# A hybrid decoder layer on one core: preparing the query weights beside four heads instead of two, and another order of the query products

## The chip, the core and the metric

The kernel runs on one core of a Trainium2 chip. The metric is device time in microseconds (us): the kernel before took 1506.83 us, the median of 3 runs (1504.25 to 1510.64). The engines are named as the profile names them: PE is TensorE (matmuls), DVE is VectorE, ACT is ScalarE, POOL is GpSimd, and SP is the engine on whose queue nearly all DMA transfers are issued.

## The reference: what is computed

One decoder layer over 1024 tokens of width 1024, in float32. Cut to what matters:

```python
h  = rmsnorm(x, ln1) @ w_in          # q, k, v and gates of all heads
m1 = mlstm_chunkwise(...)            # 4 heads of width 128, after a causal convolution and silu
m2 = forgetting_attention(...)       # 8 heads of width 64
x  = x + concat(m1 * out_gate, m2) @ w_out
h  = rmsnorm(x, ln_x)
q  = h @ w_xq                        # 4 heads of width 256
k, v = split(rmsnorm(mem, ln_mem) @ w_kv)          # 256 memory tokens
x  = x + (softmax(q @ k.T / 16) @ v) @ w_xo
x  = rmsnorm(x + relu(rmsnorm(x) @ w1) ** 2 @ w2)
```

The change touches two places: the mLSTM heads, beside which the weights w_xq are prepared, and the stretch from q to the first tiles of the product with w_xo.

## The kernel before, in words

**Precision and tiles.** Every float32 operand is split into a high and a low part (`split`, lines 141 and 142: ACT copies the high part, DVE subtracts the low one; with a scale, lines 144 and 145), and a product takes three matmuls (`mm3`, lines 195 to 197). A full tile of the output, 128 x 512, takes 8 x 3 = 24 matmuls. The accumulator banks are named mm, tp, m2 (the profile writes m), sc and ov. A bank must be evacuated, mostly by DVE, before the next product may start in it. Working tiles come from pools with few buffers: `w4` (5 buffers of 128 x 1024), `act` (7 of 128 x 4096 values, which `quarters` cuts into four of 128 x 1024), `w2` (half tiles with a letter each; r_a has one buffer only), and the weights' wr (2 buffers), wh and wl (3 each).

**Order.** The order of instructions on PE, ACT, DVE and POOL is set by a scheduler from the program's order, and each engine then takes its instructions strictly in that order. SP issues its DMAs in order as well, so an issue that waits for a buffer holds up those behind it.

**The query weights.** The product q = h @ w_xq is taken by a scheme with seven products of quarters instead of eight. For it, sums and differences of the quarters of the weights are formed ahead of time, split, and kept in DRAM (`leftd`). `query_parts(c, kh)` does this for one of eight parts (c is the head, 0 to 3, kh a half of the rows) in two phases: first two loads of w_xq (L701), a split of three quarters (128 x 768) and two stores (L706); then four additions of 128 x 256 (L711), a split of 128 x 1024, and two stores (L715). `ml_project(hd)` projects one mLSTM head and calls four parts' phases in between, in heads 1 and 3 only (the list `ahead`); heads 0 and 2 have none.

**The mLSTM head.** Its projections run one after the other on PE (convolution of k, `fx_project(0, hd)` for the attention's queries, `carried`, convolution of q, `fx_project(1, hd)`, `carry`, output gate), while the head before it is closed piece by piece (`closing`). To close it, a factor for each of its 1024 tokens is computed on DVE (c_fac, to line 673), transposed on PE, stored to DRAM (`facd`, L273) and loaded again, broadcast to all partitions, in two halves (r_a, L275 and L683); line 686 multiplies by it. `fx_project` evacuates its bank in line 724 (r_p).

**The query stage.** A list, `plan`, written out by hand, gives the order of: the loads of left operands (`L`), the query products `C(c, i)` (line 195 on; twelve matmuls each, i from 1 to 7; sums are formed on DVE in line 1281, into r_d, r_e, r_f and r_p, and a bank is used by several of these products in turn), the splitting of the right operands (`cut_right`, `cut_fourth` with the subtractions of line 1254), the loads of the memory's keys and values (`K`), the folding of a sum of squares into the factors of the second norm (`rsqrt_sums`: two additions in line 250, then four matmuls in line 253), the attention over the memory (`X`), and the start of the product with w_xo. The sums of squares themselves are formed by accumulating DMAs on POOL's queue (row<-r_c, line 1229), one for each tile of the stage before.

**The start of w_xo.** The attention's results of heads 0 to 2 go to DRAM (osd) and are loaded and split as operands (`os_load`, `os_split`). `begin_xo(n)` starts output tile n with the 18 matmuls of the six chunks that are there; `end_xo` adds the six of the last head. Three tiles are begun, in banks mm, m2 and sc. Others are computed in one go (`first_half`).

## Time and profile before

| what | value |
|---|---|
| device time, median of 3 runs | 1506.83 us (1504.25 to 1510.64) |
| the profiled execution | 1506.87 us |
| its span, from first to last instruction | 1505.1 us |
| granted clock of PE, mean | 0.995 |
| PE busy | 1481.2 us (98%) |
| DVE busy | 1140.3 us (76%) |
| ACT busy | 739.3 us (49%) |

Times in the views count from the start of the span; the execution's own time is 1.8 us longer. The projections of the mLSTM heads lie at about 65 to 345 us, the query products up to about 745 us (the last sum of line 1281 at 745.4), and the first output tiles from 749 us on. A row of waits names the engine, the line that waited, what it waited for, and the time. In a timeline, brackets behind a row hold the idle time before it and who ended it. The granted clock is 1.00 where PE runs at full speed.

### The profile page before, as it was taken

Reading aid. Unit: us, or ns where it says so; the run is one execution under the profiler, and the core shown is the slowest. Engines: PE = TensorE matmul, PEld = TensorE weight load, DVE = VectorE, ACT = ScalarE, POOL = GpSimd, SP = SyncE. Lnnn points to the kernel's source line nnn. Section 1 sums busy time; section 2 is a strip of 40 time slices with the busy share of each in tenths; the row PEclk is TensorE's granted clock in tenths of the full one; section 3 lists DMA queues with packets and bytes.
Section 4 is the critical chain, followed back from the end, with each engine's and each line's share of the span. In section 5 each row is a group of like instructions: output and inputs, shape, how many; then the busy total and the mean of one; then the engine's idle time right before and its main releaser. Section 6 shows DMA issues by size and latency. Waiting matters only on the chain.

```text
span 1505.1 us, 22082 instructions
## 1 busy us (share of the span) xinstructions
PE 1481.2 (98%) x7620; PEld 1241.3 (82%) x7620; DVE 1140.3 (76%) x1844; ACT 739.3 (49%) x1385; POOL 455.0 (30%) x545
## 2 busy tenths in 40 slices
PE   9999999999999999999999999999999999999997
PEld 8888788889999888778878788788887788888887
DVE  7687787976798875663468988888877788777765
ACT  7343344444688764533454556665656332222134
POOL 0002031313466552111110043443443653343312
PEclk9999999999999999999999999999999999999998
DMA  6345744687989768965656447767776965555623
GB/s 210 109 146 163 229 148 151 224 265 202 291 246 269 207 214 305 332 195 162 213 179 204 140 146 249 264 248 269 266 246 241 347 251 217 223 223 224 252 84 112
DMA packets 142116, 326.11 MB, mean 217 GB/s; under 512 B 15522, under 2 KB 44508, under 8 KB 136116
## 3 DMA queue, kind: packets, MB, share of 16 engines
q1 hardware_dynamic: 139700, 320.92, 62.9%
q0 software_dynamic: 2016, 3.67, 1.4%
q8 instruction: 60, 0.98, 0.3%
q14 instruction: 52, 0.43, 0.1%
q10 hardware_dynamic: 288, 0.11, 0.0%
HBM read 208.52 MB, written 112.45 MB: 213 GB/s over the span
## 4 chain that ended last, share of the span: by engine, by line
PE 77%; DMA 9%; DVE 7%; ACT 3%; issue 3%; POOL 1%; SPq 1%; POOLq 0%; DVEq 0%; ACTq 0%
PE tp L195 6%; PE tp L196 6%; PE tp L197 6%; PE sc L195 6%; PE sc L196 6%; PE sc L197 6%; PE mm L195 5%; PE mm L196 5%; PE mm L197 5%; PE m L195 5%; PE m L196 5%; PE m L197 5%; PE ov L899 2%; PE tp L879 2%; PE ov L195 2%
## 5 line engine op out<-in xcount | busy, mean ns | idle before, releaser
L195 PE MATMUL tp<-act,wl 128*128 128x512 f32 (+1 forms) x440 | 172.3, 392 | 2.5 <-DVE wl L142 1.3
L196 PE MATMUL tp<-act,wh 128*128 128x512 f32 (+1 forms) x440 | 172.3, 392 | 0.0
L197 PE MATMUL tp<-act,wh 128*128 128x512 f32 (+1 forms) x440 | 171.7, 391 | 0.0
L141 ACT ACTIVATE wh<-wr 128x1024 fp32r<-128x1024 f32 (+3 forms) x80 | 75.6, 946 | 76.0 <-PE tp L197 28.2
L195 PE MATMUL mm<-act,wl 128*128 128x512 f32 (+1 forms) x284 | 109.1, 384 | 3.1 <-DVE r_p L724 2.6
L196 PE MATMUL mm<-act,wh 128*128 128x512 f32 (+1 forms) x280 | 107.4, 383 | 0.5 <-DVE act L142 0.5
L197 PE MATMUL mm<-act,wh 128*128 128x512 f32 (+1 forms) x280 | 107.2, 383 | 0.0
L196 PE MATMUL sc<-act,wh 128*128 128x512 f32 (+1 forms) x276 | 106.8, 387 | 0.0
L197 PE MATMUL sc<-act,wh 128*128 128x512 f32 (+1 forms) x276 | 106.8, 387 | 0.0
L195 PE MATMUL sc<-act,wl 128*128 128x512 f32 (+1 forms) x268 | 104.1, 388 | 0.0
L196 PE MATMUL m<-act,wh 128*128 128x512 f32 (+1 forms) x268 | 102.0, 380 | 0.0
L197 PE MATMUL m<-act,wh 128*128 128x512 f32 (+1 forms) x268 | 101.8, 380 | 0.0
L195 PEld LDWEIGHTS tp<-act,wl 128*128 128x128 f32 x440 | 82.7, 188 | 22.4 <-ACT row L1664 1.7
L142 DVE TENSOR_TENSOR wl<-wr,wh 128x1024 fp32r<-128x1024 f32 (+3 forms) x80 | 91.7, 1147 | 11.5 <-ACT wh L141 11.4
L197 PEld LDWEIGHTS tp<-act,wh 128*128 128x128 f32 x440 | 82.7, 188 | 19.1
L196 PEld LDWEIGHTS tp<-act,wh 128*128 128x128 f32 x440 | 82.7, 188 | 18.6
L1741 POOL TENSOR_TENSOR z<-wr 128x256 f32<-128x256 f32 x56 | 54.2, 989 | 143.2 <-DMA wr<-w_ff2q 70.2
L195 PE MATMUL m<-act,wl 128*128 128x512 f32 (+1 forms) x256 | 97.5, 381 | 0.0
L141 ACT ACTIVATE w<-wr 128x768 fp32r<-128x768 f32 (+2 forms) x31 | 25.5, 824 | 130.4 <-PE tp L197 69.0
L141 ACT ACTIVATE wh<-z 128x1024 fp32r<-128x1024 f32 (+2 forms) x55 | 52.5, 957 | 64.2 <-POOL z L1741 32.2
L142 DVE TENSOR_TENSOR wl<-z,wh 128x1024 fp32r<-128x1024 f32 (+2 forms) x55 | 66.9, 1219 | 12.3 <-ACT wh L141 12.3
L195 PEld LDWEIGHTS mm<-act,wl 128*128 128x128 f32 x284 | 53.7, 189 | 14.3 <-DVE r_p L724 3.0
(789 smaller groups left out, 4413.8 us busy)
## 6 DMA issues: line engine op xcount, KB each, us to landing
act<-right SPq DMA_DIRECT2D x35, 1024.0 KB
right<-r_d SPq DMA_DIRECT2D x70, 256.0 KB
right<-w SPq DMA_DIRECT2D x56, 256.0 KB
wr<-w_ff2q SPq DMA_DIRECT2D x28, 512.0 KB
act<-fqk SPq DMA_DIRECT2D x48, 256.0 KB
wr<-w_in SPq DMA_DIRECT2D x20, 512.0 KB
wr<-w_ff SPq DMA_DIRECT2D x20, 512.0 KB
fqk<-r_p SPq DMA_DIRECT2D x32, 256.0 KB
```

Of the source, the lines that this page charges most:

```text
L141: s.activation(hi, src, AF.Copy)
L142: return v.tensor_tensor(out=lo, in0=src, in1=hi.bitcast(F32), op=ALU.subtract)
L195: nc.tensor.matmul(ps, w[1], x[0], start=first, stop=False, skip_group_check=more)
L196: nc.tensor.matmul(ps, w[0], x[1], start=False, stop=False, skip_group_check=more)
L197: nc.tensor.matmul(ps, w[0], x[0], start=False, stop=last, skip_group_check=more)
L879: nc.tensor.transpose(self.ps[:, d * P : (d + 1) * P], self.pts[d][:, self.j * P : (self.j + 1) * P], ident)
L899: nc.tensor.matmul(self.ov[:, c0:], self.fv[:, self.j], t[:, c0:], start=self.j == 0 and t is self.p[1], stop=self.last and t is self.p[0])
L1741: g.tensor_tensor(out=o, in0=x, in1=y, op=op)
```

## The change

Three edits. First, every head now carries two parts of the query weights in four phases: one inside `fx_project(0, hd)`, between its two tiles, one behind it, one behind `fx_project(1, hd)`, and one between the two tiles of the output gate. Even heads take the four working tiles of a part out of one act tile (`quarters`), odd heads take four w4 tiles. Second, the plan takes the products of the first two heads in turn, (0, 3), (1, 3), (0, 6), then cut_fourth, (1, 6), (0, 7), (1, 7), with the foldings of the two sums behind (0, 7) and (1, 7), and some loads and attention steps move by a place or two. Third, two output tiles are begun, not three; the third is computed in one go after them.

```diff
-    def query_parts(c, kh):
-
-        r = w4()
+    def query_parts(c, kh, rooms):
+
+        r, hi, lo, hs = rooms()
...
-    def fx_project(which, n):
+    def fx_project(which, n, between=lambda: None):
...
+            if hf == 0:
+                between()
...
-        ahead = [query_parts(*divmod(4 * (hd // 2) + i, 2)) for i in range(4)] if hd % 2 else []
-
-        def step(i):
-            if ahead:
-                next(ahead[i])
+        rooms = (lambda: [w4() for _ in range(4)]) if hd % 2 else quarters
+        ahead = [x for kh in range(2) for x in [query_parts(hd, kh, rooms)] * 2]
+
+        def step():
+            next(ahead.pop(0))
...
-        fx_project(0, hd)
+        fx_project(0, hd, step)
+        step()
         next(closing, None)
         parts = carried(hd, yk)
-        step(0)
         next(closing, None)
         state = []
         yq = conv_silu(hd, *q, lambda: state.extend(states(hd, *parts)))
-        step(0)
-        step(1)
         fx_project(1, hd)
-        step(1)
-        step(2)
+        step()
         sums = carry(hd, q, yq, *state)
-        step(2)
-        step(3)
...
-        step(3)
+            if hf == 0:
+                step()
```

Of the plan, the lines that matter here:

```diff
-        *C((0, 3)), O(cut_fourth), *C((1, 3)), K(0, 0, "wh"), K(0, 1, "wl"), O(rsqrt_sums, second_acc[0], rcol[:, 0:4], 4, 1, None, None, rsqrt_cols, True), *C((0, 6)), O(rsqrt_sums, second_acc[1], rcol[:, 4:8], 4, 1, None, None, rsqrt_cols, True), *C((0, 7)),
-        *C((0, 4)), L(2, 1, "wr"), X(0, 1), *C((1, 6)), L(2, 2, "wr"), L(2, 6, "wh"),
+        *C((0, 3), (1, 3)), K(0, 0, "wh"), K(0, 1, "wl"), *C((0, 6)), O(cut_fourth), *C((1, 6), (0, 7)), O(rsqrt_sums, second_acc[0], rcol[:, 0:4], 4, 1, None, None, rsqrt_cols, True), *C((1, 7)), O(rsqrt_sums, second_acc[1], rcol[:, 4:8], 4, 1, None, None, rsqrt_cols, True),
+        *C((0, 4)), L(2, 1, "wr"), X(0, 1), L(2, 2, "wr"), L(2, 6, "wh"),
...
-        O(begin_xo, 0), X(3, 0), X(3, 1), O(begin_xo, 1), X(3, 0), O(begin_xo, 2), X(3, 1), O(end_xo, 0), X(3, 1), O(end_xo, 1), O(end_xo, 2), *S(1, 0, 2, 4),
+        O(begin_xo, 0), X(3, 0), X(3, 1), O(begin_xo, 1), X(3, 0), X(3, 1), O(end_xo, 0), X(3, 1), O(end_xo, 1), O(first_half, 2), *S(1, 0, 2, 4),
```

The line numbers of the change are one to four lower behind the first edits (724 becomes 723, 1254 becomes 1251, 1281 becomes 1278). At three places the order of DVE is needed later.

DVE in head 1, around the two multiplications by the reloaded factors (L686, r_a) and the evacuation of bank mm (r_p<-mm); z is the convolution, before:

```order
L546 SCALAR_TENSOR_TENSOR z_223_1723<-z_215_1641,vec,z_223_1723 128x1024
L593 SCALAR_TENSOR_TENSOR r_p_1669<-r_p_1669,c_mx_1593 128x128
L546 SCALAR_TENSOR_TENSOR z_223_1723<-z_215_1641,vec,z_223_1723 128x1024
L686 SCALAR_TENSOR_TENSOR r_f_1207<-r_f_1207,vec,r_a_1507 128x512
L546 SCALAR_TENSOR_TENSOR z_223_1723<-z_215_1641,vec,z_223_1723 128x1024
L687 SCALAR_TENSOR_TENSOR r_f_1207<-w_140_1230,r_f_1207 128x512
L724 SCALAR_TENSOR_TENSOR r_p_1781<-mm_1756,row 128x512
L142 TENSOR_TENSOR wl_2179<-wr_2176,wh_2178 128x1024
L591 TENSOR_TENSOR r_p_1669<-sc_1681,r_p_1669 128x128
L686 SCALAR_TENSOR_TENSOR r_f_1208<-r_f_1208,vec,r_a_1590 128x512
```

And with the change:

```order
L686 SCALAR_TENSOR_TENSOR r_f_1229<-r_f_1229,vec,r_a_1537 128x512
L546 SCALAR_TENSOR_TENSOR z_226_1762<-z_218_1680,vec,z_226_1762 128x1024
L593 SCALAR_TENSOR_TENSOR r_p_1708<-r_p_1708,c_mx_1641 128x128
L687 SCALAR_TENSOR_TENSOR r_f_1229<-w_142_1252,r_f_1229 128x512
L591 TENSOR_TENSOR r_p_1708<-sc_1720,r_p_1708 128x128
L686 SCALAR_TENSOR_TENSOR r_f_1230<-r_f_1230,vec,r_a_1638 128x512
L593 SCALAR_TENSOR_TENSOR r_p_1708<-r_p_1708,c_mx_1641 128x128
L549 SCALAR_TENSOR_TENSOR z_226_1762<-z_218_1680,z_226_1762 128x1024
L145 SCALAR_TENSOR_TENSOR r_f_1229<-r_f_1229,r_y_1633 128x512
L687 SCALAR_TENSOR_TENSOR r_f_1230<-w_142_1252,r_f_1230 128x512
L723 SCALAR_TENSOR_TENSOR r_p_1802<-mm_1777,row 128x512
```

The evacuation stood behind the first of the two multiplications and ahead of the second; now it stands behind both. The last phase of query parts that stood ahead of these rows, and that of the next part, are gone from here.

DVE in the query stage, around the evacuation of bank mm after product (0, 6) (r_d<-mm) and the two subtractions of cut_fourth (w<-act) with their splits, before:

```order
L1254 TENSOR_TENSOR w_1378_7595<-act_4004 128x1024
L1254 TENSOR_TENSOR w_1379_7596<-act_4004 128x1024
L142 TENSOR_TENSOR act_7576<-w_1260_6938,act_7576 128x1024
L145 SCALAR_TENSOR_TENSOR w_1366_7530<-sc_7443,w_1366_7530 128x512
L142 TENSOR_TENSOR act_7599<-w_1378_7595,act_7599 128x1024
L142 TENSOR_TENSOR act_7599<-w_1379_7596,act_7599 128x1024
L1281 TENSOR_TENSOR r_d_7593<-sc_7537,r_p_7328 128x512
L1281 TENSOR_TENSOR r_d_7593<-mm_7635,r_d_7593 128x512
```

And with the change:

```order
L1278 TENSOR_TENSOR r_e_7538<-sc_7525,r_p_7316 128x512
L142 TENSOR_TENSOR act_7540<-act_3992,act_7540 128x1024
L142 TENSOR_TENSOR act_7564<-w_1248_6926,act_7564 128x1024
L145 SCALAR_TENSOR_TENSOR w_1354_7518<-sc_7431,w_1354_7518 128x512
L1278 TENSOR_TENSOR r_d_7581<-sc_7525,r_p_7316 128x512
L1278 TENSOR_TENSOR r_d_7581<-mm_7601,r_d_7581 128x512
L1278 TENSOR_TENSOR r_e_7558<-ov_7545,r_p_7444 128x512
L1251 TENSOR_TENSOR w_1371_7618<-act_3992 128x1024
L1251 TENSOR_TENSOR w_1372_7619<-act_3992 128x1024
```

The two subtractions stand behind the evacuation now, and the splits of what they form behind them.

DVE a few rows on, around the evacuation of bank m2 after product (1, 6) (r_d<-m) and the fold of the second sum (L250), before:

```order
L1281 TENSOR_TENSOR r_e_7550<-mm_7635,r_e_7550 128x512
L145 SCALAR_TENSOR_TENSOR w_1394_7678<-r_e_7550,w_1394_7678 128x512
L1281 TENSOR_TENSOR r_d_7616<-ov_7557,r_p_7456 128x512
L1281 TENSOR_TENSOR r_d_7616<-m_1403_7742,r_d_7616 128x512
L250 TENSOR_TENSOR row<-row 64x256 x2
L1281 TENSOR_TENSOR r_p_7328<-mm_7635,r_p_7328 128x512
```

And with the change:

```order
L1278 TENSOR_TENSOR r_d_7595<-ov_7545,r_p_7444 128x512
L250 TENSOR_TENSOR row<-row 64x256
L1278 TENSOR_TENSOR r_d_7595<-m_1374_7627,r_d_7595 128x512
L250 TENSOR_TENSOR row<-row 64x256
L145 SCALAR_TENSOR_TENSOR w_1375_7641<-r_d_7595,w_1375_7641 128x512
```

Both folds stood behind that evacuation; now the first of them stands ahead of it. On PE, product (1, 7), which uses bank m2 next, came behind product (0, 4) and 18 matmuls of scores; now it comes behind (0, 4) and four small matmuls, and the 18 come after it.

More of the change, by code (lines that the diff above doesn't have):

```diff
@@ L701, in query_parts @@
             load(q[:, 2 - 2 * e : 4 - 2 * e], a["w_xq"][2 * c + e].rearrange("p (j h c) -> h p j c", j=2, h=2)[kh])
-        hi, lo = w4(dt=F32R), w4()
+        hi, hs = hi.bitcast(F32R), hs.bitcast(F32R)
         x = slice(QC, 4 * QC)
@@ L1598, in hybrid_layer @@
-        O(begin_xo, 0), X(3, 0), X(3, 1), O(begin_xo, 1), X(3, 0), O(begin_xo, 2), X(3, 1), O(end_xo, 0), X(3, 1), O(end_xo, 1), O(end_xo, 2), *S(1, 0, 2, 4),
+        X(2, 0), *C((3, 2)), O(os_load, 0, slice(0, 4)), L(3, 4, "wr"), X(2, 1), L(3, 5, "wh"), X(2, 0), *C((3, 6)), L(3, 3, "wl"), O(os_load, 0, slice(4, 6)), X(2, 1), *C((3, 7)), K(3, 0, "w4"), *S(0, 0, 2), *C((3, 4)), K(3, 1, "w4"), *C((3, 5)), *S(0, 4), X(3, 0), *C((3, 3)), X(2, 1), O(os_load, 1, slice(0, 6)),
+        O(begin_xo, 0), X(3, 0), X(3, 1), O(begin_xo, 1), X(3, 0), X(3, 1), O(end_xo, 0), X(3, 1), O(end_xo, 1), O(first_half, 2), *S(1, 0, 2, 4),
```

4 lines of the change are left out of this document (1 added, 3 removed).

## The prediction

> **What bounds the kernel now.** I read the page's head first, then the waits of PE (TensorE), then PE's idle time and clock by stretch, and last the timelines of the engines that PE waited for.
>
> ```profile
> span 1505.1 us, 22082 instructions
> PE 1481.2 (98%) x7620; PEld 1241.3 (82%) x7620; DVE 1140.3 (76%) x1844; ACT 739.3 (49%) x1385; POOL 455.0 (30%) x545
> ```
>
> PE is busy for all but 24 us, and the change leaves its matmuls as they are in number and shape. So the change can only take away, add or move PE's idle time, and the lower clock that may follow idle time. PE's waits name where that is (microseconds in all, times, longest):
>
> ```profile
> PE mm L195 <- DVE r_d L1281: 2.6, 1, 2.6
> PE mm L195 <- DVE r_p L724: 2.6, 1, 2.6
> PE sc L195 <- DVE r_e L142: 2.1, 1, 2.1
> PE tp L195 <- DVE wl L142: 1.3, 1, 1.3
> PE mm L195 <- ACT act L141: 0.6, 1, 0.6
> PE mm L195 <- DVE r_f L616: 0.5, 1, 0.5
> PE mm L196 <- DVE act L142: 0.5, 1, 0.5
> ```
>
> The second, third and sixth of these lie in the mLSTM stage (183, 328 and 341 us), the first in the query stage (653 us), the others where the output tiles of the attention over the memory begin (749 to 781 us). All seven are 10.2 us. By stretch (window; then busy time and count of PE, PEld, DVE, ACT and POOL; granted clock; DMA share; GB/s):
>
> ```profile
> 175.00:200.00 25.00, 22.44 (x103) 18.32 (x102) 19.66 (x30) 12.50 (x22) 3.88 (x5) 0.93 0.60 208
> 325.00:350.00 25.00, 22.24 (x182) 21.38 (x181) 20.61 (x32) 13.47 (x26) 13.11 (x18) 1.00 0.84 248
> 650.00:675.00 25.00, 22.35 (x111) 18.63 (x111) 15.36 (x33) 7.38 (x18) 3.76 (x5) 0.93 0.61 173
> ```
>
> Two stretches have a granted clock of 0.93, which is 1.75 us lost in 25. PE's own rows show the same at 653.77: twelve matmuls up to 658.21, and the next twelve up to 661.01.
>
> ```profile
> 653.77 0.50 PE L195 MATMUL mm<-act,wh 128*128 128x512 f32 x1 [2.65 <-DVE r_d L1281]
> 658.21 0.40 PE L195 MATMUL ov<-act,wl 128*128 128x512 f32 x1
> 661.01 0.28 PE L195 MATMUL sc<-wh,w 128*128 128x256 f32 x1
> ```
>
> The first twelve took 4.44 us, the next 2.80 (0.233 each): 1.64 us is clock. So the two waits of 2.6 us cost about 4.3 us each (2.6 and 1.6 to 1.75), and the one of 2.1 us, with a clock of 1.00 in its stretch, only 2.1.
>
> The Trainium skill (TensorE: Matmul & The Clock Gate, section "Why this matters for your kernels") says that there should be "No PE-idle gaps >~3µs between matmul bursts", and that an idle window of about 3.4 us (section "What's actually happening") halves the clock. By that rule gaps of 2.6 us would lose no clock, and the two waits would be worth 5.2 us together, not 8.6; the trace decides against it, with 1.64 us lost behind a gap of 2.65.
>
> **Part 1: query parts beside all four mLSTM heads.** Each part of the query weights costs two DMA loads, ACT copies, VectorE (DVE) subtractions and two stores. Busy time and mean ns of one, 120 to 340 us:
>
> ```profile
> L711 DVE TENSOR_TENSOR w<-w 128x256 f32<-128x256 f32 x32 | 13.5, 422 | 0.5
> L142 DVE TENSOR_TENSOR w<-w,w 128x1024 f32<-128x1024 f32 x8 | 9.8, 1219 | 0.0
> L142 DVE TENSOR_TENSOR w<-w,w 128x768 f32<-128x768 f32 x8 | 8.0, 999 | 9.6 <-ACT w L141 4.5 <-DMA leftd<-w 3.4 <-ACT r_d L141 1.6
> L141 ACT ACTIVATE w<-w 128x768 fp32r<-128x768 f32 x8 | 6.8, 845 | 13.2 <-DMA w<-w_xq 13.2
> ```
>
> One part is 4 x 0.42 + 1.22 + 1.00 = 3.9 us of DVE. Before, heads 1 and 3 each carry four parts (15.6 us) and heads 0 and 2 none; now each head carries two (7.8 us). No work is added. What the crowding did in head 1 stands in SP's and DVE's timelines, with the same transfers in head 2, which has no parts, as the last two rows:
>
> ```profile
> 171.59 0.43 SPq L273 DMA_DIRECT2D facd<-r_a  x1
> 176.90 0.34 SPq L275 DMA_DIRECT2D r_a<-facd  x1
> 180.87 0.33 SPq L683 DMA_DIRECT2D r_a<-facd  x1
> ```
>
> ```profile
> 180.09 0.75 DVE L686 SCALAR_TENSOR_TENSOR r_f<-r_f,vec,r_a 128x512 f32<-128x512 f32 x1 [3.09 <-DMA r_a<-facd]
> 182.56 0.68 DVE L724 SCALAR_TENSOR_TENSOR r_p<-mm,row 128x512 f32<-128x512 f32 x1
> ```
>
> ```profile
> 235.09 0.29 SPq L273 DMA_DIRECT2D facd<-r_a  x1
> 236.35 0.32 SPq L275 DMA_DIRECT2D r_a<-facd  x1
> ```
>
> A 4 KB store of the factors (facd) took 5.3 us until its reload could be issued in head 1, and 1.3 us in head 2. DVE, which goes in order, stood 3.09 us for the reload, and the evacuation of bank mm behind it (L724, done 183.24) is what PE waited for. In head 3 it is the load of a query weight that ACT waits for (5.4 us in two waits), then DVE, then PE at 328:
>
> ```profile
> ACT w L141 <- DMA w<-w_xq: 5.4, 2, 4.7
> ```
>
> In the new order of DVE the evacuation (L723) stands further back: behind both reloads of the factors, not one (rows of before and of the change are given ahead). So it is not simply earlier. With T as the time when the first reload lands, it is done at T + 0.75 (L686), then about 4.0 for the second reload (issue 180.87 behind the first L686 in the rows above, 3.2 us from issue to landing as for the first: 176.90 to 180.09), then some 4.0 of DVE (L686 0.75, L593 0.3, L549 1.2, L145 0.7, L687 and L723 0.7 each, less overlaps): T + 8. PE reaches the matmul at about 180.7 (183.29 less 2.56). The factors are transposed on PE 25 matmuls sooner (5.8 us), so the store goes out at about 165 to 166; with a way of 1.3 to 5.3 us and 3.2 us for the reload, T is 170 to 174, and the evacuation is done at 178 to 182. I take 180: no stall, or one too short to touch the clock. That is -4.3 us (ends 0 and -4.3).
>
> In head 3 two parts fewer lie ahead of the wait at 328: -2.1 (ends 0 and -2.1). The 0.5 us at 341 I leave.
>
> Heads 0 and 2 get what they never had: 7.8 us of DVE, four w_xq loads on SP's queue each, in a tile that the gates of head 0 must release first. DVE's room there:
>
> ```profile
> 100.00:125.00 25.00, 25.00 (x122) 20.66 (x121) 17.64 (x32) 10.51 (x19) 3.36 (x4) 1.00 0.38 112
> 225.00:250.00 25.00, 25.00 (x119) 20.49 (x118) 20.72 (x42) 8.31 (x15) 2.03 (x3) 1.00 0.42 132
> ```
>
> 7.4 us free in 25 in head 0, 4.3 in head 2, and the head is about 65 us long, so the work fits by sum, yet delays what stands behind it by 1 to 4 us. I put +1 us of small waits on PE (ends 0 and +8.6, two waits as long as head 1's). Part 1: -4.3 - 2.1 + 1 = -5.4.
>
> **Part 2: the query products alternate.** The wait at 653.77 is for the evacuation of bank mm after product (0, 6):
>
> ```profile
> 645.95 2.36 DVE L1254 TENSOR_TENSOR w<-act 128x1024 f32<-128x1024 f32 x2
> 649.96 2.35 DVE L142 TENSOR_TENSOR act<-w,act 128x1024 fp32r<-128x1024 f32 x2
> 652.23 0.69 DVE L1281 TENSOR_TENSOR r_d<-sc,r_p 128x512 f32<-128x512 f32 x1
> 653.02 0.69 DVE L1281 TENSOR_TENSOR r_d<-mm,r_d 128x512 f32<-128x512 f32 x1
> 661.94 0.69 DVE L1281 TENSOR_TENSOR r_d<-m,r_d 128x512 f32<-128x512 f32 x1
> 664.01 0.88 DVE L250 TENSOR_TENSOR row<-row 64x256 f32<-64x256 f32 x2 [1.38 <-DMA row<-r_c]
> ```
>
> The order shows the 2.36 + 2.35 us of cut_fourth behind this evacuation now. Without them it would be done at 653.7 - 4.6 = 649.1, but product (0, 6) ends seven matmuls before PE's need at 651.1 (653.77 less 2.65), at 649.5, so it is done at about 650.2, and the wait goes: -4.3.
>
> But something takes its place. In the new order the first fold of the second row sum (L250) stands ahead of the evacuation of bank m2 (r_d<-m), and product (1, 7), which needs that bank, comes directly behind (0, 4), no longer behind 18 score matmuls. The fold waits for the last of a chain of accumulating DMAs on POOL's queue, each of which waits for the one before:
>
> ```profile
> 658.10 0.85 POOL L1229 DMA_DIRECT2D row<-r_c  x1 [4.21 <-DMA row<-r_c]
> ```
>
> This chain does not run faster because PE does. PE reaches (1, 7) at 651.1 + 2.8 for (0, 7) + 2.8 for (1, 3) + 9 x 0.12 for scores + 2.8 for (0, 4) + 0.3 = 660.9. The bank is free at 664.0 + 0.42 + 0.69 = 665.1: a wait of 4.2 us, longer than both that lost clock, so 1.6 us more. From there 2.8 for (1, 7), 18 x 0.12 and 0.3 lead to 670.4, or 672.0 with the clock, where before PE was at the same matmul (start of product (2, 1)) at 670.7. Part 2: +1.3 (ends -4.3, if the chain lands 4 us sooner, and +2.5, if it lands a microsecond later).
>
> **Part 3: two output tiles begun, not three.** PE's waits at 749.49 and 750.75 are for the split of the loaded products on ACT and DVE:
>
> ```profile
> 748.38 2.01 ACT L141 ACTIVATE act<-act 128x1024 fp32r<-128x1024 f32 x2 [3.84 <-DMA act<-osd]
> ```
>
> ```profile
> 749.47 1.22 DVE L142 TENSOR_TENSOR act<-act,act 128x1024 fp32r<-128x1024 f32 x1 [2.23 <-ACT act L141]
> ```
>
> Now the first twelve matmuls of the first tile come about 2 us sooner after the last stored product, and the load stands one weight transfer sooner on SP's queue. These offset each other, and I keep a wait of 0.5 to 1. The 1.3 us at 781 (a weight split behind others on DVE) becomes about 0.3, since its tile comes later; the closing heads' last transposes get some 6 us less cover, which may cost 0.5. Part 3: -0.5 (ends -2.4, all waits gone, and +4.3, one long wait).
>
> **Sum.** -5.4 + 1.3 - 0.5 = -4.6 us. The profiled execution took 1506.87 us (span 1505.1 and 1.8 around it), the median is 1506.83, so the forecast is 1502 us for both. Half a per cent, 7.5 us, is about what a measurement of this kernel can tell from no change.
>
> **The rivals.**
> - A, the query gain stays: the fold is not late for (1, 7), because the accumulating chain, which starts with PE's stage, ends sooner. For it: the landings differ (4.2 to 5.1 us of waiting each). Against it: it must gain 4 us in the last 40. It gives -5.4 - 4.3 - 0.5 = -10.2: 1497 us. Chance 0.22.
> - B, head 1's wait stays, now behind the second reload, and head 3's too: decided by T above 172.7. It gives +1 + 1.3 - 0.5 = +1.8: 1508 us. Chance 0.22.
> - C, slower: heads 0 and 2 now wait as head 1 did. DVE stands in order at the first subtraction of a part until the w_xq load has landed and ACT has copied it (3.7 to 4.7 us as in head 3); beyond the 1 to 2 us that PE's next need leaves, each costs up to 4.3 with the clock. Two of them and B: 8.6 + 1.3 - 0.5 = +9.4: 1516 us. Chance 0.1.
> - D, the start of the output tiles gets one wait of 2.6 us with its clock: +4.3 on the forecast, 1506 us. Chance 0.06.
>
> The forecast keeps 0.4, with 1498 to 1506 of its own. From 1494 to 1511 leaves out C and the best half of A with the ends of part 3: about 0.2. Faster by over 0.5% holds most of A and a little of the forecast: 0.27. Slower holds C and an edge of B: 0.13. Within: 0.6.
>
> **What would show it.** Right: no PE wait on r_p L723 near 180 us, none on r_e L142 near 326; DVE's r_d<-mm at about 650 (less the gain before it); a new PE wait of about 4 us on r_d L1278 with bank m, behind L250 and the last row<-r_c, and a clock under 1 there. Wrong: DVE waits on w_xq in heads 0 and 2 with PE waits behind them; PE at product (2, 1) more than 2 us sooner after product (0, 6) than before; a wait over 2 us at the first output tile.

## The result, and the profile after

The changed kernel took 1514.12 us (median of 9 runs, 1511.36 to 1521.14), the kernel before 1505.96 us beside it: a ratio of 1.0057, 95% interval 1.0039 to 1.0075. The forecast was 1502 us with a range up to 1511, so the sign was wrong and the range too narrow. Three later measurements of the same kernel, on three chips, gave ratios of 1.0026, 1.0035 and 1.0055, so its loss is real and its size, 0.26% to 0.57%, differs. The mean of the four is 0.43%, some 6.5 us.

The head of the profile after:

```profile
span 1513.6 us, 22093 instructions
PE 1484.1 (98%) x7620; PEld 1242.5 (82%) x7620; DVE 1145.8 (76%) x1844; ACT 739.0 (49%) x1385; POOL 464.5 (31%) x545
```

The span is 8.5 us longer and PE is busy for 2.9 us more with the same 7620 matmuls; the rest is idle time. PE's waits after (microseconds in all, times, longest):

```profile
PE ov L195 <- DVE r_e L1278: 4.8, 1, 4.8
PE ov L196 <- DVE r_e L142: 3.3, 4, 2.5
PE sc L837 <- ACT act L850: 2.3, 2, 1.5
...
PE mm L195 <- DVE wl L142: 1.5, 1, 1.5
PE mm L195 <- ACT act L141: 1.5, 1, 1.5
...
PE sc L195 <- DVE r_c L641: 0.9, 1, 0.9
PE tp L195 <- DVE wl L142: 0.9, 1, 0.9
PE sc L195 <- DVE r_f L616: 0.9, 1, 0.9
```

The waits of 2.6 us on r_p (183 us) and r_d (653 us) are gone, and that on r_e L142 at 328 us is now one of 0.9 on r_f. In their place stand 4.8 us on a sum r_e in the query stage, 2.5 us on a split r_e at 341 us, and 1.5 us twice in the stretch of the output tiles (at 753 and 790 us). By stretch (window; busy time and count of PE, PEld, DVE, ACT, POOL; granted clock; DMA share; GB/s):

```profile
175.00:200.00 25.00, 25.00 (x131) 21.17 (x130) 20.07 (x32) 15.66 (x28) 10.23 (x13) 1.00 0.74 231
325.00:350.00 25.00, 21.51 (x164) 20.64 (x163) 17.54 (x25) 9.95 (x19) 11.43 (x14) 0.93 0.58 162
650.00:675.00 25.00, 20.25 (x92) 16.57 (x90) 13.59 (x23) 4.94 (x7) 3.60 (x4) 0.86 0.62 162
750.00:775.00 25.00, 22.56 (x113) 18.28 (x112) 14.25 (x23) 14.63 (x31) 3.69 (x8) 0.93 0.45 152
```

The first stretch is now full, as forecast. The other three have idle time and a clock of 0.86 to 0.93.

**Where the time came from.** PE takes the same matmuls in both kernels, so the time between two of them can be compared. The table takes PE's instructions by their number, from the start of one to the start of the other, at numbers where both kernels have the same kind of work. All profiled executions of a kind are put together, those of the experiments below too, since single ones differ: "before" and "changed" mean the order that the stretch has, whatever the other stretches do. Microseconds, mean, lowest and highest:

| PE's instructions | what lies there | before | changed | difference |
|---|---|---|---|---|
| 600 to 920 | mLSTM head 0 | 64.16 (6 executions, 64.15 to 64.16) | 65.5 (11, 64.15 to 67.05) | +1.4 |
| 920 to 1500 | heads 1 and 2 | 118.6 (6, 117.5 to 120.1) | 115.9 (11, 115.8 to 116.3) | -2.7 |
| 1500 to 2200 | head 3 and its closing | 108.3 (5, 107.1 to 110.4) | 110.4 (9, 109.3 to 111.4) | +2.1 |
| 3600 to 4125 | query products | 110.3 (3, 109.3 to 111.1) | 112.6 (9, 109.5 to 116.1) | +2.2 |
| 4125 to 5000 | rest of the attention, first output tiles | 194.6 (2, 194.2 and 195.0) | 197.4 (6, 196.1 to 198.7) | +2.8 |

Kernels with an edit, or a third order of PE's instructions, in a stretch are left out of its row, and what the table leaves out differs by less than 0.5 us in the mean. The sum is +5.8 us, near the 6.5 us of the four measurements. One stretch gained; four lost. The ranges are apart in two rows only, heads 1 and 2 and the last one; in the others they overlap, so a difference of 1 to 2 us there is one of means and does not show in every execution.

**Head 1 went as worked out.** SP, then DVE:

```profile
167.33 0.29 SPq L273 DMA_DIRECT2D facd<-r_a  x1
168.55 0.32 SPq L275 DMA_DIRECT2D r_a<-facd  x1
...
173.67 0.32 SPq L683 DMA_DIRECT2D r_a<-facd  x1
```

```profile
172.89 0.75 DVE L686 SCALAR_TENSOR_TENSOR r_f<-r_f,vec,r_a 128x512 f32<-128x512 f32 x1 [1.27 <-DMA r_a<-facd]
...
176.70 0.75 DVE L686 SCALAR_TENSOR_TENSOR r_f<-r_f,vec,r_a 128x512 f32<-128x512 f32 x1 [0.80 <-DMA r_a<-facd]
...
179.97 0.68 DVE L723 SCALAR_TENSOR_TENSOR r_p<-mm,row 128x512 f32<-128x512 f32 x1
```

The store's way is 1.2 us, not 5.3; T is 172.9, and the evacuation is done at 180.65, T + 7.8. PE did not wait.

**Head 3 got another wait.** First two splits on DVE in the kernel before, then DVE, POOL and PE of the changed kernel:

```profile
342.70 1.83 DVE L142 TENSOR_TENSOR r_e<-r_c,r_d 128x512 fp32r<-128x512 f32 x2
```

```profile
337.09 4.34 DVE L142 TENSOR_TENSOR r_e<-r_c,r_d 128x512 fp32r<-128x512 f32 x2
```

```profile
338.11 2.77 POOL L646 TENSOR_TENSOR r_b<-r_c,r_b 128x256 f32<-128x256 f32 x4
```

```profile
341.48 0.39 PE L196 MATMUL ov<-r_e,act 128*128 128x256 f32 x1 [2.50 <-DVE r_e L142]
```

Two splits that take 1.83 us in the kernel before took 4.34 us, and ended half a microsecond after POOL's four additions of line 646. PE stood 2.5 us and lost clock. All nine executions with this order and POOL's additions have the wait (2.50 to 2.53 us); in five of them the clock fell with it.

**The query stage was late two products sooner than I had it.** POOL, ACT and DVE of the changed kernel:

```profile
651.68 0.85 POOL L1226 DMA_DIRECT2D row<-r_c  x1 [5.78 <-DMA row<-r_c]
660.19 0.84 POOL L1226 DMA_DIRECT2D row<-r_c  x1 [7.66 <-DMA row<-r_c]
663.95 0.86 POOL L1226 DMA_DIRECT2D row<-r_c  x1 [2.92 <-DMA row<-r_c]
```

```profile
659.75 0.63 ACT L1224 ACTIVATE r_c<-r_e 128x512 f32<-128x512 f32 x1 [7.88 <-DMA row<-r_c]
```

```profile
660.41 0.69 DVE L1278 TENSOR_TENSOR r_e<-ov,r_p 128x512 f32<-128x512 f32 x1 [7.66 <-ACT r_c L1224]
...
667.48 0.42 DVE L250 TENSOR_TENSOR row<-row 64x256 f32<-64x256 f32 x1
667.82 0.68 DVE L1278 TENSOR_TENSOR r_d<-m,r_d 128x512 f32<-128x512 f32 x1
```

ACT's square needs a free r_c, and both were held for accumulating DMAs, one under way and one waiting its turn on POOL's queue; the square reads the old r_e; DVE's new r_e must wait for the square; and product (1, 3) needs bank ov, which that sum empties. PE waited 4.75 us for it and then ran its twelve matmuls at about half clock, in 5.1 us where twelve take 2.8. The fold (L250) that the prediction had watched came 7 us later without a wait. In the kernel before the same square and sum ran at 652.60 and 653.63, the sum without a wait:

```profile
652.60 0.63 ACT L1227 ACTIVATE r_c<-r_e 128x512 f32<-128x512 f32 x1 [1.67 <-DMA row<-r_c]
```

**The first output tile waited.** SP, ACT and PE of the changed kernel:

```profile
742.76 0.33 SPq L183 DMA_DIRECT2D wr<-w_xo  x1
743.91 0.32 SPq L1553 DMA_DIRECT2D act<-osd  x1
```

```profile
752.43 2.00 ACT L141 ACTIVATE act<-act 128x1024 fp32r<-128x1024 f32 x2 [4.95 <-DMA act<-osd]
```

```profile
753.53 0.50 PE L195 MATMUL mm<-act,wl 128*128 128x512 f32 x1 [1.45 <-ACT act L141]
...
754.79 0.77 PE L196 MATMUL mm<-act,wh 128*128 128x512 f32 x1 [0.76 <-DVE act L142]
```

The load of the stored products took 8.5 us, from issue to ACT's start, behind a weight's load that was issued 1.15 us ahead of it. In the kernel before it was nearly as slow, 8.2 us behind a weight's load issued 1.45 us ahead, but there PE had score products to run meanwhile and waited 0.6 and 0.5 us. Why the weight stands ahead of it is shown by the last experiments.

### The profile page after: what moved, and what is told of

It reads as the page before. It is cut to its first block, busy times and chain, and to the rows that moved or that the text cites. A ratio compares the mean times of both kernels' runs of the same rounds, so it can differ in the third digit from the quotient of the medians.

```text
span 1513.6 us, 22093 instructions
## 1 busy us (share of the span) xinstructions
PE 1484.1 (98%) x7620; PEld 1242.5 (82%) x7620; DVE 1145.8 (76%) x1844; ACT 739.0 (49%) x1385; POOL 464.5 (31%) x545
## 4 chain that ended last, share of the span: by engine, by line
PE 77%; DMA 11%; DVE 6%; ACT 3%; issue 2%; POOL 1%; SPq 1%; POOLq 0%; DVEq 0%; ACTq 0%
PE tp L195 7%; PE tp L196 7%; PE tp L197 7%; PE sc L195 6%; PE sc L196 6%; PE sc L197 6%; PE m L195 4%; PE m L196 4%; PE m L197 4%; PE mm L196 4%; PE mm L197 4%; PE mm L195 4%; DMA row<-r_c 3%; PE ov L896 2%; PE ov L196 2%
## 5 line engine op out<-in xcount | busy, mean ns | idle before, releaser
L195 PE MATMUL tp<-act,wl 128*128 128x512 f32 (+1 forms) x456 | 178.4, 392 | 0.9 <-DVE wl L142 0.9
L196 PE MATMUL tp<-act,wh 128*128 128x512 f32 (+1 forms) x456 | 178.7, 392 | 0.0
L197 PE MATMUL tp<-act,wh 128*128 128x512 f32 (+1 forms) x456 | 178.2, 392 | 0.0
L196 PE MATMUL sc<-act,wh 128*128 128x512 f32 (+1 forms) x268 | 103.7, 387 | 0.0
L197 PE MATMUL sc<-act,wh 128*128 128x512 f32 (+1 forms) x268 | 103.7, 387 | 0.0
L142 DVE TENSOR_TENSOR wl<-wr,wh 128x1024 fp32r<-128x1024 f32 (+3 forms) x80 | 91.2, 1141 | 16.4 <-ACT wh L141 15.4
L197 PEld LDWEIGHTS tp<-act,wh 128*128 128x128 f32 x456 | 85.7, 188 | 19.7
L196 PEld LDWEIGHTS tp<-act,wh 128*128 128x128 f32 x456 | 85.7, 188 | 19.2
L195 PE MATMUL sc<-act,wl 128*128 128x512 f32 (+1 forms) x260 | 100.8, 388 | 0.0
L1738 POOL TENSOR_TENSOR z<-wr 128x256 f32<-128x256 f32 x56 | 55.5, 1011 | 141.6 <-DMA wr<-w_ff2q 128.5
L197 PE MATMUL m<-act,wh 128*128 128x512 f32 (+1 forms) x260 | 98.9, 380 | 0.0
L196 PE MATMUL m<-act,wh 128*128 128x512 f32 (+1 forms) x260 | 98.8, 380 | 0.0
L195 PE MATMUL m<-act,wl 128*128 128x512 f32 (+1 forms) x248 | 94.2, 380 | 0.0
L142 DVE TENSOR_TENSOR wl<-z,wh 128x1024 fp32r<-128x1024 f32 (+2 forms) x55 | 68.9, 1255 | 11.6 <-ACT wh L141 11.5
L142 DVE TENSOR_TENSOR r_e<-tp,r_d 128x512 fp32r<-128x512 f32 (+2 forms) x81 | 47.8, 592 | 24.1 <-ACT r_d L141 22.8
```

The costliest lines, as they stand in the source:

```text
L142: return v.tensor_tensor(out=lo, in0=src, in1=hi.bitcast(F32), op=ALU.subtract)
L195: nc.tensor.matmul(ps, w[1], x[0], start=first, stop=False, skip_group_check=more)
L196: nc.tensor.matmul(ps, w[0], x[1], start=False, stop=False, skip_group_check=more)
L197: nc.tensor.matmul(ps, w[0], x[0], start=False, stop=last, skip_group_check=more)
L1738: g.tensor_tensor(out=o, in0=x, in1=y, op=op)
```

## The experiments

Ratios are to the kernel before on the same chip, with their 95% intervals. The runs have the names e1 to e15, and nearly keep their order, since later ones answer what earlier ones left.

**Parts alone.** The first three kernels are the change with the old plan (part 1), and the kernel before with the plan's lines for the query products (part 2) or for the output tiles (part 3):

```diff
 # e1_part1: the changed kernel, plan of before
-        *C((0, 3), (1, 3)), ..., *C((0, 6)), O(cut_fourth), *C((1, 6), (0, 7)), ...
+        *C((0, 3)), O(cut_fourth), *C((1, 3)), ..., *C((0, 6)), ..., *C((0, 7)),
 # e2_part2: the kernel before
-        *C((0, 3)), O(cut_fourth), *C((1, 3)), ..., *C((0, 6)), ..., *C((0, 7)),
+        *C((0, 3), (1, 3)), ..., *C((0, 6)), O(cut_fourth), *C((1, 6), (0, 7)), ...
 # e3_part3: the kernel before
-        L(3, 4, "wr"), X(2, 0), X(2, 1), *C((3, 2)), O(os_load, 0, slice(0, 4)), L(3, 5, "wh"), ...
+        X(2, 0), *C((3, 2)), O(os_load, 0, slice(0, 4)), L(3, 4, "wr"), X(2, 1), L(3, 5, "wh"), ...
-        ... O(begin_xo, 2), X(3, 1), O(end_xo, 0), X(3, 1), O(end_xo, 1), O(end_xo, 2), ...
+        ... X(3, 1), O(end_xo, 0), X(3, 1), O(end_xo, 1), O(first_half, 2), ...
```

> Part 1 alone: the query parts beside all four heads, with the plan of before. My theory after the two traces (each part costs by itself): the waits at 183 and 328 us go (4.2 and 2.1 us less), new waits come in head 0 (2.6 us, on DVE's sums and splits behind a query part) and in head 3 (2.5 us and its clock, about 341 us), and the start of the memory weights in the attention gives 1.3 more: +0 to +2.5 us against before, with PE at the end of the mLSTM stage within 1.5 us of before. Rival (the prediction's own sum for this part): about -5 us.

Measured: 1505.54 us, ratio 1.0006 (0.9994 to 1.0019). Part 1 gained nothing: the wait at 183 us was gone, but one of 2.5 us at 341 us and one of 1.0 us in head 0, whose stretch took 2.8 us longer, had come.

> Part 2 alone: the changed order of the query products, all else as before. My theory: the wait of 2.65 us before product (0, 7) goes, and one of 3 to 5 us with its clock comes before product (1, 3), since DVE's evacuation of bank ov into r_e waits for the square on ACT that still reads r_e, and that for the accumulating DMA that still reads r_c; and since this order also brings the first output tile forward by 2 us, it has the longer wait there as well: +4 to +7 us. Rival 1: the accumulating DMA of 8 us that caused it was chance; then the query stretch gains 2 to 4 us and the sum is -1 to +2. Rival 2 (the prediction's): a wait before product (1, 7), behind the fold, and +1.3.

Measured: 1507.09 us, ratio 1.0012 (0.9993 to 1.0030). Here the wait that the prediction described did come, for the bank of product (1, 7):

```profile
666.81 0.79 PE L195 MATMUL m<-act,wh 128*128 128x512 f32 x1 [2.68 <-DVE r_d L1281]
```

It was 2.7 us long, not 4.2. The first output tile had a wait of 2.0 us as well.

> Part 3 alone: two output tiles begun, and the load of (3, 4) two places later in the plan, all else as before. By the order PE's instructions differ only behind the last scores, from the third tile on. My theory: the wait at the first output tile stays at 0.5 to 1.2 us, since that tile is no sooner; the transposes of the last head get less cover: 0.2 to 1 us; sum 0 to +1.5 us. Rival: dropping the third tile is what makes the first output tiles wait in the changed kernel: +3 to +4.

Measured: 1504.26 us, ratio 0.9995 (0.9983 to 1.0008). Added up, the parts give +0.9 + 1.8 - 0.8 = +1.9 us. Each has an interval of 2 to 3 us to either side, so this points to a loss that the parts have only in company, without showing it yet.

**The accumulating chain (e4).** In the changed kernel, the square is added by POOL itself, in place of a DMA that accumulates:

```diff
-            g.dma_start(second_acc[hf], sq, accum_op=ALU.add)
+            g.tensor_tensor(out=second_acc[hf], in0=sq, in1=second_acc[hf], op=ALU.add)
```

> The changed kernel, with the sums of squares added up by POOL itself in place of the accumulating DMAs on its queue. My theory: squares and r_e come free within 2 to 3 us, so the wait of 4.75 us before product (1, 3) and its 2.6 us of clock go, and none comes before (1, 7): 6 to 8 us less than the changed kernel. Rival (the wait is for something else, or the additions on POOL hold up DVE): the changed kernel's time within 2 us.

Measured: 1498.15 us, ratio 0.9962 (0.9947 to 0.9977). POOL's rows show what stands for the chain now:

```profile
633.42 1.74 POOL L1226 TENSOR_TENSOR row<-r_c,row 128x512 f32<-128x512 f32 x1 [4.48 <-ACT r_c L1224]
635.51 1.36 POOL L1226 TENSOR_TENSOR row<-r_c,row 128x512 f32<-128x512 f32 x1 [0.35 <-ACT r_c L1224]
```

An addition takes 1.3 to 1.7 us, where an accumulating DMA of the profile after took 3.2 to 8.0 us from issue to landing. The query stretch fell from 112.6 to 104.8 us, and PE's wait in it was gone. This kernel is not a pure test, though. The scheduler, which now has work to place on POOL, moved query products and scores in that stretch as well; it also put the first twelve products of the output tiles back behind the last eighteen score products, and that stretch fell by 2.9 us too.

**The same kernel again (e5), and parts 2 and 3 together (e6).** The second is the kernel before with all the plan's lines of the change; both ran on another chip:

> The changed kernel once more, for a second trace. My theory: the wait of PE before product (1, 3) on r_e comes again, 3 us or more with its clock, and 1512 to 1516 us. Rival: the accumulating DMA of 8 us just ahead of it was chance; then this wait is under 2 us or PE waits before (1, 7) instead, as in the run of part 2 alone, and the time is 1508 to 1511.

Measured: 1507.51 us, ratio 1.0026 (1.0010 to 1.0042). This is below both ranges that were expected. PE's wait for r_e at the query products came again, 2.1 us long; the load act<-osd took 7.1 us, and the first output tile waited only 0.8 us, for DVE's split of what it brought.

> Parts 2 and 3 without part 1; PE's order from the query stage on is that of the changed kernel. The parts alone sum to 2 us, the whole costs 8. My theory: parts 2 and 3 together bring the first output tile forward in PE's order (neither does so fully alone), so most of the missing 6 us is in this pair: +5 to +7 us against before. Rival: part 1 makes it, by the phase in which PE meets the accumulating DMAs; then the pair is +1 to +2.

Measured: 1509.38 us, ratio 1.0035 (1.0021 to 1.0049). So parts 2 and 3 hold the loss: +5.3 us together, while +1.8 and -0.8 alone, and +3.9 for the whole change on this chip.

**Another buffer for the late sum (e7).** In the changed kernel, the second head's sum takes r_f, which no square reads:

```diff
-            u["22"] = w2("e" if c < 2 else "f")
+            u["22"] = w2("f" if c else "e")
```

> The changed kernel, with the sum that product (1, 5) starts held in an r_f tile and not in r_e, so that it doesn't wait for the last square, which still reads r_e; the scheduler then also moves the evacuation r_d<-m ahead of the fold and (1, 3) and (1, 7) forward. My theory: the wait of 4.75 us and its clock go (7 us less in the query stage) and only the output tiles' waits stay: 1506 to 1509 us. Rival (the chain of accumulating DMAs sets the pace anyhow, through the fold): the wait comes back a product later at about the same size, and the time is within 2 us of the changed kernel's.

Measured: 1509.07 us, ratio 1.0034 (1.0021 to 1.0048). PE's wait for r_e had gone, and a longer one stood behind the fold, at 669 us (6.5 us; PE's waits, then DVE's fold):

```profile
PE mm L196 <- DVE act L142: 6.8, 2, 6.5
```

```profile
667.46 0.42 DVE L250 TENSOR_TENSOR row<-row 64x256 f32<-64x256 f32 x1 [8.12 <-DMA row<-r_c]
```

The split that PE waited for stands behind this fold on DVE. With another buffer the chain is caught in another place, at about the same price, as the rival had it.

**The addition on POOL in the kernel before (e8).** The edit is e4's, made there:

> The kernel before, with the sums of squares added by POOL in place of the accumulating DMAs. My theory: the chain was hidden before (the fold's wait of 1.4 us lay on DVE), the wait of 2.65 us before (0, 7) has another cause, DVE's own order: within 2 us of before, and 4 to 7 us behind the changed kernel with the same edit (1498). Rival: most of that kernel's gain over before comes from POOL's additions alone: 1498 to 1500.

Measured: 1503.55 us, ratio 0.9994 (0.9981 to 1.0007). The kernel before gains nothing from POOL's addition that the runs can tell. Its trace is no good witness: the profiled execution took 1498.46 us, the lowest of its runs. Still, in the two traces of the kernel before with this edit (e8, and e13 below) the query stretch takes 105.6 and 106.1 us, against 110.3 without it, and 104.8 in both traces of the changed kernel with it (e4, e10). So with the squares on POOL the two plans are about 1 us apart in that stretch, far from the 4.3 us that the forecast saw in the wait at 653 us. The edit moves PE's order there in both plans, so what of this is the chain and what the order stays open.

**POOL's four additions in head 3 (e9).** In the changed kernel, for the last head alone:

```diff
-                        g.tensor_tensor(out=acc[:, x], in0=wt[:, z], in1=acc[:, x], op=ALU.add)
+                        (v if hd == MLH - 1 else g).tensor_tensor(out=acc[:, x], in0=wt[:, z], in1=acc[:, x], op=ALU.add)
```

> The changed kernel with the four small additions per weight part of line 646 made by VectorE, not GpSimd, for the last mLSTM head alone. In the changed kernel's execution VectorE's split (L142) at 337.09 took 4.34 us for its two operations while GpSimd ran four of these additions back to back, and TensorE then waited 2.505 us at 341.48 with a granted clock of 0.93 in that stretch. Theory (VectorE is held by GpSimd's four additions): the pair of L142 goes back to about 1.8 us, the 2.5-us wait goes and its clock loss with it, so 2.5 to 4 us below the changed kernel of the same job, from which four additions of about 0.7 us more on VectorE may take up to 1 us. Rival (the wait stands for something else that is late there): a wait of 1.5 us or more stays before the same matmuls, and the time is within 1 us of the changed kernel's.

Measured: 1507.50 us, ratio 1.0018 (1.0006 to 1.0031), 3.2 us below the changed kernel on this chip (1510.74, below). On DVE the additions cost 0.4 us each and the splits are back at 0.69 (DVE's timeline, then the stretch):

```profile
333.31 0.41 DVE L646 TENSOR_TENSOR r_b<-r_c,r_b 128x256 f32<-128x256 f32 x1
333.64 0.69 DVE L142 TENSOR_TENSOR r_e<-r_c,r_d 128x512 fp32r<-128x512 f32 x1
334.24 0.42 DVE L646 TENSOR_TENSOR r_b<-r_c,r_b 128x256 f32<-128x256 f32 x1
334.58 0.69 DVE L142 TENSOR_TENSOR r_e<-r_c,r_d 128x512 fp32r<-128x512 f32 x1
```

```profile
325.00:350.00 25.00, 24.95 (x213) 24.65 (x212) 18.00 (x41) 10.96 (x24) 8.36 (x9) 1.00 0.62 170
```

The 2.5-us wait and its clock are gone. The theory holds: POOL's additions held up DVE's split. (The scheduler moved some of PE's instructions in this stretch as well.)

**Both edits in the changed kernel (e10)**, e4's and e9's:

> The changed kernel with both edits: the sum of squares added by GpSimd itself in place of the accumulating DMA (which alone gave a ratio of 0.9962), and the additions of line 646 of the last mLSTM head on VectorE. Theory: the two causes lie in different stages, 200 us apart, so the gains add up: some 2.5 to 4 us below the ratio of 0.9962, that is 0.993 to 0.995 of the kernel before, 1494 to 1496 us. Rival: the gain of the additions is taken back by a later stage (the first output tiles or the closing), and the ratio stays at 0.996.

Measured: 1495.55 us, ratio 0.9934 (0.9917 to 0.9951). This version is 10 us below the kernel before and 15 below the changed kernel on the same chip.

**Parts 1 and 2 without part 3 (e11), and the changed kernel on the same chip (e12):**

> Parts 1 and 2 of the change without part 3: the weight load that part 3 moves back stands where it stood, and three output tiles are begun, not two. In what TensorE runs, the twelve first products of the output tiles stand ahead of the last eighteen score products here as in the changed kernel, and the chain of accumulating DMAs is as there. Theory (what the change loses lies in part 2 with the accumulating chain and in the place of those twelve products, not in the count of tiles begun): within 2 us of the changed kernel of the same job, with a wait for r_e or r_d of 2 to 5 us at the query products. Rival (part 3 is what turns part 2 from a wash into a loss): about the time of parts 1 and 2 alone added up, +1 to +3 us on the kernel before, and 3 us or more below the changed kernel of the same job.

Measured: 1507.09 us, ratio 1.0011 (0.9995 to 1.0027), 3.6 us below the changed kernel on this chip. The rival's numbers came out: part 3 does matter beside part 2, though alone it cost nothing that the runs can tell, and my theory of what the change loses was too small. The last stretch of the table was 193.95 us, 3.4 below the changed kernel's, and act<-osd took 5.5 us.

> The changed kernel once more, on the chip of the three others, since its loss was 0.57% on one chip and 0.26% on another. If the loss comes from the accumulating chain whose length differs with the chip and the execution, it lies again between 0.2% and 0.6%, and the wait for r_e at the query products between 2 and 5 us goes with its size. If the first 0.57% was a disturbance of that job, it is at 0.2 to 0.3%.

Measured: 1510.74 us, ratio 1.0035 (1.0020 to 1.0050), with 5.0 us of wait for r_e.

**What of part 3 it is (e14, and the changed kernel beside it, e15).** Part 3 holds two moves: the third tile, and the load L(3, 4). The second stood in the prediction only as "one weight transfer". This kernel is the changed one with the load alone put back:

```diff
-        X(2, 0), *C((3, 2)), O(os_load, 0, slice(0, 4)), L(3, 4, "wr"), X(2, 1), L(3, 5, "wh"), ...
+        L(3, 4, "wr"), X(2, 0), X(2, 1), *C((3, 2)), O(os_load, 0, slice(0, 4)), L(3, 5, "wh"), ...
```

> The changed kernel with one load (L(3, 4)) back ahead of the attention step and of the loading of the stored products, where it was before; still two output tiles begun. On SyncE's queue the load act<-osd then stands ahead of the load of a w_xo weight, not behind it. In the changed kernel's executions act<-osd took 8.3 to 8.5 us behind that weight, in the execution with parts 1 and 2 alone 5.5 us with nothing ahead of it. Theory (this one move of a load is what part 3 costs): act<-osd lands about 3 us sooner, the two waits of 1.5 and 0.8 us at the first output tile and their clock loss shrink to under 1 us, and the time is 2.5 to 4 us below the changed kernel of the same job. Rival (it is the third tile that is not begun): the waits go but come back later, and the time is within 1.5 us of the changed kernel.

Measured: 1504.24 us, ratio 1.0002 (0.9991 to 1.0013), with the changed kernel beside it:

> The changed kernel, beside the two others on the same chip, as the measure for them: 0.2% to 0.6% above the kernel before, with the 2 to 5 us of wait for r_e at the query products, the 2.5 us at 341 us, and two waits of about 1.4 and 0.8 us where the first output tile begins.

Measured: 1512.90 us, ratio 1.0055 (1.0038 to 1.0071). One load's place is worth 8.7 us between these medians, with intervals far apart, and more than I expected; against the mean of the changed kernel's four ratios, 1.0043, it is 6 us. With the load the scheduler moved some instructions of PE, ACT and DVE in the last stretch of the table; the first twelve matmuls of the output tiles stay ahead of the last eighteen score products. SP and ACT of the kernel with the load put back:

```profile
740.39 0.32 SPq L1553 DMA_DIRECT2D act<-osd  x1
740.80 0.38 SPq L183 DMA_DIRECT2D wr<-w_xo  x1
```

```profile
745.66 2.01 ACT L141 ACTIVATE act<-act 128x1024 fp32r<-128x1024 f32 x2 [2.76 <-DMA act<-osd]
```

And of the changed kernel on the same chip:

```profile
741.78 0.33 SPq L183 DMA_DIRECT2D wr<-w_xo  x1
742.91 0.32 SPq L1553 DMA_DIRECT2D act<-osd  x1
```

```profile
751.60 2.00 ACT L141 ACTIVATE act<-act 128x1024 fp32r<-128x1024 f32 x2 [4.92 <-DMA act<-osd]
```

The two loads have changed places. Ahead of the weight, act<-osd takes 5.3 us from issue to ACT's start; behind it, 8.7. The stretches show that the delay does not end at the first tile (first the kernel with the load put back, then the changed one, with one of its waits):

```profile
750.00:775.00 25.00, 24.01 (x131) 20.13 (x131) 14.40 (x26) 14.22 (x32) 3.70 (x8) 1.00 0.64 219
775.00:800.00 25.00, 25.00 (x109) 20.13 (x108) 23.27 (x31) 15.04 (x21) 0.00 (x0) 1.00 0.61 208
```

```profile
750.00:775.00 25.00, 22.41 (x115) 18.25 (x114) 14.26 (x23) 14.73 (x32) 3.71 (x8) 0.93 0.44 144
775.00:800.00 25.00, 21.81 (x92) 16.45 (x91) 16.05 (x21) 13.15 (x19) 0.00 (x0) 1.00 0.61 209
```

```profile
PE mm L195 <- DVE wl L142: 2.2, 1, 2.2
```

In these 50 us PE is idle for 1.0 us and 5.8 us, besides a clock of 0.93 in the first 25 of the latter. Of the 5.8 us, 3.0 are two waits for splits of w_xo weights, at 790 us (the row) and 798 us, which the kernel with the load put back does not have. The whole stretch (PE's instructions 4125 to 5000) took 191.39 us with the load put back and 198.69 without: 7.3 us of the 8.7. It is also 3.2 us shorter than in the kernel before (194.6), and 2.6 shorter than in e11 (193.95), which has the early load and three tiles. That would be the gain of beginning two tiles when the load is in time, but it rests on one execution each.

**The two edits in the kernel before (e13):**

> The kernel before, with its own plan, and the two edits that made the changed kernel fast: the squares added by GpSimd in place of the accumulating DMAs, and the last mLSTM head's small additions of line 646 on VectorE. The changed kernel with both had a ratio of 0.9934. Theory (the change's own gains are real and were covered by the two costs): the kernel before gains little from the two edits, 0.997 to 0.999, so that the change is worth about 0.4 to 0.6% once both costs are gone. Rival (the two edits are the whole gain, the change is worth nothing): 0.993 to 0.995 here too.

Measured: 1500.10 us, ratio 0.9973 (0.9963 to 0.9984), against 0.9934 (0.9917 to 0.9951) for the changed kernel with the same edits. So with both hidden costs gone, the changed kernel is about 0.4% ahead, measured on different chips, a little more than the 4.6 us that the forecast had. It is not the worth of the plan alone: at the first output tile the edits move PE's order in opposite ways, the first twelve products ahead of the last eighteen score products in e13, behind them in e10.

## Why the prediction was wrong, point by point

**Part 1, -5.4 forecast, about +0.8 by the table, +0.9 measured alone.**
- Head 1, -4.3: the mechanism was right, T + 8 within 0.2 us, and the wait never came back. The size failed, by the step "the two waits of 2.6 us cost about 4.3 us each": it was one execution's. In the six executions with the old order PE waited there 2.56, 2.39, 1.70, 1.21, 1.18 and 1.03 us, and the clock fell with the first alone, which is the one that the forecast read. In the mean heads 1 and 2 gained 2.7 us.
- Head 3, -2.1: failed. "The 0.5 us at 341 I leave" is the step. The wait at 328 went down to 0.9 us, but POOL's four additions then fell on DVE's second split, 2.5 us of wait, in five of nine executions with a lower clock. e9 showed it by moving the additions; with them on DVE the stretch took 106.4 and 106.0 us (e9, e10), about 2 us less than the 108.3 before. That this is near the forecast -2.1 is in part luck, since the wait that goes was 2.1 us in the forecast's trace and 0.4 to 1.5 in the other five with the old order.
- Heads 0 and 2, +1: about right; +1.4, all in head 0, and 0 to 2.9 us from one execution to the next. Rival C's place was right, its size was not. In the profile after DVE stood 2.0 us at 125 us for ACT's copy behind a w_xq load, as C has it, and PE waited 0.9 us at 128.5; in e5 DVE stood 2.3 us there and PE did not wait.

**Part 2, +1.3 forecast, +2.2 by the table, +1.8 measured alone.** That the wait at 653 goes, that the chain of accumulating DMAs does not run faster because PE does, and that its end takes the wait's place, all held: the rows above tie PE's wait to the chain step by step, e7 moved the wait to the fold, and in e4 it was gone. What failed is where it is caught: I followed the fold's row and not the buffers of the squares (r_c) and of the sums that they read (r_e), which stand two products ahead of it. The wait came before (1, 3), 4.75 us and about 2.3 us of clock, where the forecast had 4.2 and 1.6 before (1, 7). In e2, alone, it was the predicted place. Rival A, an earlier chain, did not occur.

**Part 3, -0.5 forecast, -0.8 measured alone, within the noise; +2.8 by the table together with part 2.** The step that failed is "These offset each other, and I keep a wait of 0.5 to 1". Two edits meet here: part 2 lets the scheduler put the first twelve products of the tiles ahead of the last eighteen score products, so PE needs act<-osd sooner, and part 3's later L(3, 4) lets a w_xo weight's load slip ahead of act<-osd on SP's queue, so it lands later than with part 2 alone. In the order of part 3 alone the score products cover the load; in the order of part 2 alone the load is early, and only a weight's split was late (2.0 us in that execution). Together nothing covers it: the load is as slow as in the kernel before, and PE waits 1.45 and 0.76 us for it and loses clock, where I kept 0.5 to 1. I counted the weight transfers ahead of the load (one, not two) and not whether the one that stayed was issued right ahead of it. Rival D named this place with 4.3 us; putting the load back gave 6 to 9.

**The chances.** The forecast's error is made of several terms: two waits of the mLSTM heads sized on the longest of six executions, a new wait in head 3 that was left out, the wait of the query stage in another place, and two terms set against each other at the first output tile. The slower case held 0.13, in a mechanism (heads 0 and 2) that was worth 1.4 us of what was lost.

Open stays why an accumulating DMA in the chain takes 3 us in one place and 8 in another, why head 0 waits in some executions and not in others of the same program, and why POOL's addition shortens the query stretch of the kernel before in two traces (e8, e13) but not the median of e8.

## What to carry to other kernels

When an edit lets a consumer run earlier, list for each buffer that its producers write who still reads it, the DMAs included, and not only the engine rows in front of it: a slow chain is caught at the first buffer that it holds. When a load moves by one place in a program, read the issuing queue's new order around the loads that PE needs next, since a bulk load issued one place ahead can cost more than the compute that was rearranged (here 6 to 9 us). And a wait read from one execution is one draw: before a forecast adds up waits of 1 to 3 us, look at how much the same stretch differs between executions.

## What the runs showed of the hardware

- DVE and POOL hold one another up over several instructions, and which one is held more goes with the start. In the ten executions where POOL's first addition of line 646 started 0.3 to 0.4 us after DVE's second split (changed order, and e2), the split took 3.65 to 3.75 us and the four additions 0.7 us each. In the four where it started before that split (the order before), the split took 1.22 to 1.23 us and the first two additions 1.0 to 1.2. With the additions on DVE the split took 0.69.
- An accumulating DMA of 128 x 512 values took 3 to 10 us from issue to landing in the 13 executions that have the chain (3.2 to 8.0 in the profile after); POOL adds the same values in 1.3 to 1.7 us (e4).
- The clock fell with some waits of PE and not with others of the same length: with one of the six of 1.0 to 2.6 us in head 1, with five of the nine of 2.5 us in head 3, with one of 2.1 us in e5 (655 us) and not with one of 2.1 us in e8 (741 us). Each time it was at half for 3.4 or 6.8 us.
- The load act<-osd took 5.2 to 6.3 us, from issue to ACT's start, in the five executions where it was issued ahead of the first w_xo weight's load; 7.1 to 8.7 us in the nine with such a load 1.1 to 1.6 us ahead of it; 4.9 to 6.4 in the three where that was 2.4 us or more.
- With the same order of PE's instructions, the stretch of mLSTM head 0 took 64.2 to 67.1 us in 11 executions (64.6 to 67.1 in the changed kernel's own four), and that of heads 1 and 2 in the old order 117.5 to 120.1 us in 6.
